# Sums of squares of each attention head's output: a row of ones as weights, or the squares as weights

## The chip, the core and the metric

One program on one NeuronCore of a Trainium2 chip; the other cores are idle. The metric is the device time of the whole program in microseconds, a median over several executions. The engines are PE (matrix multiply, with its weight loads shown apart as PEld), DVE (vector), ACT (scalar activation), POOL (GpSimd) and SP (which issues DMAs); each works through its own queue in order, and semaphores tie them together.

## The reference

One encoder layer on 1024 tokens of width 1024: RMSNorm, a combined projection into a pooling branch and eight heads of differential attention, gates, an output projection, and an MLP with squared ReLU. What matters here is the end of attention:

```python
o = lax.map(block, (q_blocks, q_pos))             # softmax0 @ v - lam * softmax1 @ v
o = o.transpose(1, 0, 2, 3, 4).reshape(B, S, N_HEADS, V_HEAD_DIM)
o = head_rmsnorm(o, g_sub) * (1.0 - lambda_init)
```

For each token and head, `head_rmsnorm` needs the mean of the squares of the head's 128 output channels. The rest of the layer is as usual:

```python
merged = (gates[..., :D_MODEL] * (y_pool @ w_branch_pool[l])
          + gates[..., D_MODEL:] * (y_attn @ w_branch_attn[l]))
x = x + merged @ w_out[l]
x = x + jnp.square(jax.nn.relu(h2 @ w_up[l])) @ w_down[l]
```

## The kernel before

All products keep fp32 accuracy by splitting each operand into a high part, rounded to the fp32r type, and a low part, the remainder (`split`, L118: a cast on ACT, a subtraction on DVE or POOL); `mm3` (L123) adds three fp32r matmuls for each product. Transposes go through PE as well, with the identity matrix `identf`.

The first 700 us are the attention stage. For each head h (8) and each tile t of 128 tokens (8), a chain of small generators runs: A makes q, k, v (`z`, 24 matmuls of 384 columns), B normalizes them, C transposes q and k, D makes the scores and the softmax, E transposes the attention weights, and for each pair p of tiles F multiplies them with v and H sums the squares. The table `ORDER` (L50, L51) interleaves the stages of neighbouring tiles in the order in which they are written; after that, the framework's scheduler lays every engine's queue out anew from its priorities and its own model of time. Matmuls of the gates and of the pooling branch (`g`, `u`) have lower priority and fill the gaps between.

`stage_pv` (L539) leaves a head's output, transposed, for 256 tokens in the PSUM bank `po`: partitions are the head's 128 channels, columns 0 to 255 one partial sum and 256 to 511 the other. There is one such bank. ACT copies the second half to `oS` (L558), DVE adds the first (L559), ACT squares it into `oq` (L560), and `oS` is stored to DRAM (L561). `split` then makes two fp32r digits `oqs` of the squares (L563).

`stage_ssq` (L567) sums over the channels, which lie on partitions, by a matmul: the weights are the 128x128 tile `ones`, the digits are streamed (L570, L571, 256 columns each), so that every partition of the second half of `po` holds the same row of 256 sums. To get them as columns, with tokens on partitions, DVE multiplies each 128x128 block with the identity and adds up along the row (L573, twice, each followed by a read of its accumulator) into the table `SS[h]`. When a head is done, `stage_norm` (L580) makes the factors from `SS[h]` and transposes and stores them; the factors are used only after the attention stage. For the last tile of the last head, H and R get a later priority (L642, L643).

From 700 us on follow the branch projections, the gates, the output projection and the MLP, the two larger ones by a Strassen-like scheme of seven products; the change doesn't touch them.

Of the kernel before, what the change touches and what calls it, by code (L numbers as in the profile page):

```python
# [9 lines left out]
F32R = mybir.dt.float32r  # L10
I32 = mybir.dt.int32
AF = mybir.ActivationFunctionType
ALU = mybir.AluOpType
# [4 lines left out]
P = 128  # L18
# [40 lines left out]
def encoder_kernel(  # L59
# [21 lines left out]
    nc = tc.nc  # L81
    x, out = x[0], out[0]
# [32 lines left out]
    def f(ap):  # L115
        return ap.bitcast(F32)

    def split(hi, lo, src, lo_eng=None):  # L118

        nc.scalar.copy(hi, src)  # L120
        return (lo_eng or nc.vector).tensor_tensor(lo, src, f(hi), op=ALU.subtract)  # L121
# [91 lines left out]
    identf = units.tile([P, P], F32, name="identf")  # L213
# [3 lines left out]
    ones = units.tile([P, P], F32R, name="ones")  # L217
# [57 lines left out]
    with ExitStack() as ph:  # L275
# [6 lines left out]
        def s1(shape, dt, name, tag, bufs=1):  # L282
            return sq_pool.tile(shape, dt, tag=tag, name=name, bufs=bufs)
# [107 lines left out]
        st = {}  # L391
        ATs = {}
        Zs = {}
        SS = {}
# [144 lines left out]
        def stage_pv(h, p):  # L539
            V, rooms = KV[h][1], ATs.pop((h, p))  # L540
            po = ps_o.tile([P, 512], F32, tag="o", name=f"po{h}_{p}")
            both = po.rearrange("p (d c) -> p d c", d=2)
            nkt = 2 * p + 2
            order = [*range(nkt - 2), nkt - 1, nkt - 2] if p else [0, 1]
            for i, kt in enumerate(order):
                v_hi, v_lo = (V[kt // 4][:, kt % 4, d, :] for d in range(2))
                a = rooms[kt // 2][:, :, kt % 2, :]
                if kt < nkt - 1:
                    nc.tensor.matmul(both, v_hi, a, start=i == 0, stop=False)
                    nc.tensor.matmul(po[:, 0:256], v_lo, a[:, 0, :], start=False, stop=i == nkt - 1)  # L550
                else:
                    for v in (v_hi, v_lo):
                        nc.tensor.matmul(both[:, :, P:256], v, a[:, :, P:256], start=False, stop=i == nkt - 1 and v is v_lo)
                if i % 2 and i < nkt - 1:
                    yield
            oS = s1([P, 256], F32, f"oS{h}_{p}", "oS", 2)
            oq = s1([P, 256], F32, f"oq{h}_{p}", "oq")
            nc.scalar.copy(oS, po[:, 256:512])  # L558
            nc.vector.tensor_tensor(oS, po[:, 0:256], oS, op=ALU.add)  # L559
            nc.scalar.activation(oq, oS, AF.Square)  # L560
            nc.scalar.dma_start(y_dram[h * P : (h + 1) * P, p * 256 : (p + 1) * 256], oS)  # L561
            oqs = s1([P, 2, 256], F32R, f"oqs{h}_{p}", "oqs")
            split(oqs[:, 0, :], oqs[:, 1, :], oq)  # L563
            st[h, p, "o"] = (po, oq, oqs)
            yield

        def stage_ssq(h, p):  # L567

            po, oq, oqs = st.pop((h, p, "o"))
            nc.tensor.matmul(po[:, 256:512], ones, oqs[:, 0, :], start=True, stop=False)  # L570
            nc.tensor.matmul(po[:, 256:512], ones, oqs[:, 1, :], start=False, stop=True)  # L571
            for i in range(2):
                nc.vector.tensor_tensor_reduce(  # L573
                    out=oq[:, i * P : (i + 1) * P], in0=po[:, 256 + i * P : 256 + (i + 1) * P], in1=identf,
                    scale=1.0, scalar=0.0, op0=ALU.mult, op1=ALU.add,
                    accum_out=SS[h][:, 2 * p + i : 2 * p + i + 1],
                )
            yield

        def stage_norm(h):  # L580
# [19 lines left out]
        def stage(w, g):  # L600
            h, t = divmod(g, NT)
            if w == "A":
                if t == 0:
                    head_start(h)
                yield from stage_qkv(h, t)
            elif w == "B":
                yield from stage_prep(h, t)
            elif w == "C":
                yield from stage_qkT(h, t)
            elif w == "D":  # L610
                yield from stage_scores(h, t)
            elif w == "E":
                yield from stage_aT(h, t)
            elif w == "F" and t % 2:
                yield from stage_pv(h, t // 2)
            elif w == "H" and t % 2:
                yield from stage_ssq(h, t // 2)
            elif w == "R" and t == NT - 1:
                yield from stage_norm(h)
            elif w == "W" and t == 0 and h:  # L620
                for kp in range(NK // 2):
                    load_w(h, kp)
                    split_w(h, kp, nc.gpsimd)

        for g in range(-2, N + 8):
# [11 lines left out]
            for tok in ORDER:  # L637
                if tok not in gens:
                    i = g - tok[1]
# [897 lines left out]
```

## Time and profile before

| | us |
|---|---|
| median of 3 executions (1526.28 to 1529.02) | 1528.49 |
| the profiled execution's own time | 1528.55 |
| its span in the trace | 1526.7 |
| PE busy | 1510.5 |
| PE weight loads (PEld) busy | 1301.4 |
| DVE busy | 1051.1 |
| ACT busy | 803.5 |
| POOL busy | 321.3 |
| first and last of the sums' matmuls (L570, L571) start at | 77.5 and 689.4 |

A row of the timeline gives the start, the time taken, the engine, the line in the program, the operation, what it writes and reads by the names of the program's tiles, and the shapes. "x4" is four in close order, whose time runs from the start of the first to the end of the last. A matmul's time includes its way through the array, which overlaps with the next one, so how far an instruction moves the next one is read from the difference of start times. A weight load (PEld) stands ahead of each matmul and can run beside the matmul before it. In the list of waits, "PE sc L484 <- DVE nm L487: 0.5, 1, 0.5" says that PE sat idle before L484 for 0.5 us in all, once, 0.5 at most, and that DVE's L487 ended it. In the view of one tile, three numbers after the count are the shortest, the median and the longest duration in ns.

### The profile page before, as it was taken

What the parts mean: (1) busy time and instruction counts of PE and PEld (TensorE: products, weight loads), DVE (VectorE), ACT (ScalarE), POOL (GpSimd) and SP (SyncE); (2) the same over time, 40 slices, a digit from 0 to 9 for tenths busy, and PEclk for the clock granted to TensorE, in tenths of its full rate; (3) what the DMA queues carried; (4) which work ended last, traced back from release to release, by engine and by line L of the source; (5) the groups of instructions that cost most, each with busy time, mean ns of one, the idle gap of its engine ahead of it and who ended that gap; (6) DMA issues with size and microseconds to landing.
All of it is one profiled execution on the core that took longest, in us unless ns stands there. A gap on an engine that the chain in (4) does not pass through costs nothing.

```text
span 1526.7 us, 21670 instructions
## 1 busy us (share of the span) xinstructions
PE 1510.5 (99%) x7441; PEld 1301.4 (85%) x7441; DVE 1051.1 (69%) x2262; ACT 803.5 (53%) x1693; POOL 321.3 (21%) x412
## 2 busy tenths in 40 slices
PE   7999999999999999999999999999999999999998
PEld 6999998999898989888888887888888888888887
DVE  7776768877777777746578569766665668556572
ACT  6665556656566565454464466555555633333331
POOL 6687333325234242312100011000000000000000
PEclk9999999999999999999999999999999999999999
DMA  8353211112112121626365734554433799537650
GB/s 247 103 161 121 72 34 57 52 42 68 43 44 84 49 98 37 226 86 242 135 207 188 253 111 140 173 178 152 151 125 111 278 363 366 166 125 262 226 193 28
DMA packets 171608, 221.07 MB, mean 145 GB/s; under 512 B 10902, under 2 KB 104811, under 8 KB 171499
## 3 DMA queue, kind: packets, MB, share of 16 engines
q1 hardware_dynamic: 154090, 192.39, 38.1%
q10 hardware_dynamic: 17408, 27.30, 4.7%
q8 instruction: 59, 0.97, 0.3%
q14 instruction: 51, 0.41, 0.1%
HBM read 157.76 MB, written 61.90 MB: 144 GB/s over the span
## 4 chain that ended last, share of the span: by engine, by line
PE 92%; DVE 4%; DMA 1%; ACT 1%; SPq 1%; issue 1%; DVEq 0%; ACTq 0%
PE z L126 6%; PE z L128 6%; PE z L127 5%; PE Da L126 4%; PE Da L128 4%; PE Da L127 4%; PE g L126 4%; PE g L127 4%; PE g L128 4%; PE Db L128 3%; PE Db L126 3%; PE Db L127 3%; PE X L128 2%; PE X L126 2%; PE X L127 2%; PE sc L484 2%
## 5 line engine op out<-in xcount | busy, mean ns | idle before, releaser
L126 PE MATMUL z<-wqkv,hT 128*128 128x384 f32 x512 | 174.7, 342 | 0.7 <-DVE qn L428 0.4
L128 PE MATMUL z<-wqkv,hT 128*128 128x384 f32 x512 | 173.7, 340 | 0.0
L127 PE MATMUL z<-wqkv,hT 128*128 128x384 f32 x512 | 173.6, 339 | 0.0
L495 ACT ACTIVATE s<-s,nm 128x256 f32<-128x256 f32 (+7 forms) x128 | 99.5, 778 | 45.9 <-DVE nm L487 45.1
L126 PE MATMUL g<-hT,fwgate 128*128 128x512 f32 x256 | 101.1, 395 | 0.1
L127 PE MATMUL g<-hT,fwgate 128*128 128x512 f32 x256 | 100.8, 394 | 0.0
L128 PE MATMUL g<-hT,fwgate 128*128 128x512 f32 x256 | 100.5, 393 | 0.0
L126 PEld LDWEIGHTS z<-wqkv,hT 128*128 128x128 f32 x512 | 96.8, 189 | 3.9 <-DVE qn L428 1.1
L127 PEld LDWEIGHTS z<-wqkv,hT 128*128 128x128 f32 x512 | 96.8, 189 | 3.0
L128 PEld LDWEIGHTS z<-wqkv,hT 128*128 128x128 f32 x512 | 96.7, 189 | 2.6 <-DVE hT L121 0.5
L235 POOL TENSOR_TENSOR ms<-ms,mhalf 128x4 f32<-128x4 f32 x64 | 65.7, 1027 | 156.6 <-DVE ms L234 133.6
L121 DVE TENSOR_TENSOR AT<-ta,AT 128x256 fp32r<-128x256 f32 (+1 forms) x160 | 62.2, 392 | 31.6 <-ACT AT L120 30.6
L487 DVE CUSTOM_DVE_ANT_0 s<-sc,dist 128x512 f32<-128x512 f32 (+3 forms) x128 | 74.0, 584 | 13.7 <-PE sc L485 12.5
L120 ACT CAST AT<-ta 128x256 fp32r<-128x256 f32 (+1 forms) x160 | 54.6, 348 | 38.4 <-PE ta L527 21.6
L484 PE MATMUL sc<-K,Q 128*128 128x512 f32 (+2 forms) x192 | 69.8, 366 | 0.6 <-DVE nm L487 0.5
L121 DVE TENSOR_TENSOR AS<-s,AS 128x512 fp32r<-128x512 f32 x64 | 45.1, 706 | 35.8 <-ACT AS L120 35.6
L485 PE MATMUL sc<-K,Q 128*128 128x512 f32 (+2 forms) x192 | 66.4, 350 | 0.0
L121 POOL TENSOR_TENSOR wqkv<-rqkv,wqkv 128x384 fp32r<-128x384 f32 x60 | 61.8, 1046 | 18.9 <-ACT wqkv L120 15.4
L121 POOL TENSOR_TENSOR fwgate<-frgate,fwgate 128x512 fp32r<-128x512 f32 x32 | 43.0, 1345 | 66.7 <-ACT fwgate L120 60.6
L126 PEld LDWEIGHTS g<-hT,fwgate 128*128 128x128 f32 x256 | 48.1, 188 | 9.4 <-ACT go L730 0.5
L128 PEld LDWEIGHTS g<-hT,fwgate 128*128 128x128 f32 x256 | 48.1, 188 | 8.9
L127 PEld LDWEIGHTS g<-hT,fwgate 128*128 128x128 f32 x256 | 48.1, 188 | 8.4
(455 smaller groups left out, 4489.7 us busy)
## 6 DMA issues: line engine op xcount, KB each, us to landing
wd<-in_w_down_dram SPq DMA_DIRECT2D x56, 512.0 KB, 5.6
wu<-in_w_up_dram SPq DMA_DIRECT2D x32, 512.0 KB, 4.7
udS<-us SPq DMA_DIRECT2D x64, 256.0 KB, 2.4
ur<-udS SPq DMA_DIRECT2D x32, 512.0 KB, 3.3
rqkv<-in_w_in_dram SPq DMA_DIRECT2D x64, 192.0 KB, 2.7
ud<-u ACTq DMA_DIRECT2D x48, 256.0 KB, 4.6
ur<-ud SPq DMA_DIRECT2D x24, 512.0 KB, 4.6
frgate<-in_w_gate_dram SPq DMA_DIRECT2D x32, 256.0 KB, 2.7
```

Source lines behind the costliest of these rows:

```text
L120: nc.scalar.copy(hi, src)
L121: return (lo_eng or nc.vector).tensor_tensor(lo, src, f(hi), op=ALU.subtract)
L126: nc.tensor.matmul(ps, lhs_hi, rhs_hi, start=first, stop=False, **kw)
L127: nc.tensor.matmul(ps, lhs_hi, rhs_lo, start=False, stop=False, **kw)
L128: nc.tensor.matmul(ps, lhs_lo, rhs_hi, start=False, stop=last, **kw)
L235: nc.gpsimd.tensor_tensor(dst, dst, mhalf[:, :n], op=ALU.pow)
L484: nc.tensor.matmul(dst, Q[:, i, 0, :], rhs, start=True, stop=False)
L485: nc.tensor.matmul(dst, Q[:, i, 1, :], rhs, start=False, stop=True)
L487: nc.vector.tensor_tensor_reduce(out=s[i][:, c : c + w], in0=sc[:, 0:w], in1=dist[:, o0 + c : o0 + c + w], scale=2.0 ** -(h + 1), scalar=B ...
L495: nc.scalar.activation(s[i][:, 0:n], s[i][:, 0:n], AF.Exp, bias=last, scale=-1.0, accum_out=Z[:, i, t : t + 1])
```

## The change

The squares `oq` are no longer split: they are used as they are, in fp32, and as the stationary operand. For each of the two tiles of a pair, one matmul has a 128x128 block of the squares as its weights and one column of `ones` (as fp32) as its moving operand. Channels are summed and tokens come out on partitions, one column for each tile, in columns 256 and 257 of `po`. One DVE copy of 128x2 moves them into `SS[h]`. The tile `oqs`, the two digits, the masked reductions and their accumulator reads are gone.

```diff
             nc.scalar.dma_start(y_dram[h * P : (h + 1) * P, p * 256 : (p + 1) * 256], oS)
-            oqs = s1([P, 2, 256], F32R, f"oqs{h}_{p}", "oqs")
-            split(oqs[:, 0, :], oqs[:, 1, :], oq)
-            st[h, p, "o"] = (po, oq, oqs)
+            st[h, p, "o"] = (po, oq)
             yield
 
         def stage_ssq(h, p):
 
-            po, oq, oqs = st.pop((h, p, "o"))
-            nc.tensor.matmul(po[:, 256:512], ones, oqs[:, 0, :], start=True, stop=False)
-            nc.tensor.matmul(po[:, 256:512], ones, oqs[:, 1, :], start=False, stop=True)
+            po, oq = st.pop((h, p, "o"))
             for i in range(2):
-                nc.vector.tensor_tensor_reduce(
-                    out=oq[:, i * P : (i + 1) * P], in0=po[:, 256 + i * P : 256 + (i + 1) * P], in1=identf,
-                    scale=1.0, scalar=0.0, op0=ALU.mult, op1=ALU.add,
-                    accum_out=SS[h][:, 2 * p + i : 2 * p + i + 1],
+                nc.tensor.matmul(
+                    po[:, 256 + i : 257 + i], oq[:, i * P : (i + 1) * P], f(ones)[:, 0:1], start=True, stop=True
                 )
+            nc.vector.tensor_copy(SS[h][:, 2 * p : 2 * p + 2], po[:, 256:258])
             yield
```

Because the scheduler sees other instructions, it lays the queues of the whole attention stage out differently. Two places show it. The first is PE at the first sum, head 0 and tiles 0 and 1 (`po_0` is the bank of that pair, `sc` a score bank, `ta` the transposed attention weights, `g` a gate, `z` a projection). Before:

```order
L128 MATMUL g_0_6794<-hT_0_0_156,fwgate_1_6791 128x512
L484 MATMUL sc_4_1_0_937<-K_0_366,Q_4_779 128x512
L485 MATMUL sc_4_1_0_937<-K_0_366,Q_4_779 128x512
L570 MATMUL po_0_803<-oqs_0_814,ones 128x256
L527 MATMUL ta_3_0_919<-identf,s_3_786 128x128 x4
L484 MATMUL sc_4_1_512_941<-K_1_367,Q_4_779 128x256
L571 MATMUL po_0_803<-oqs_0_814,ones 128x256
L485 MATMUL sc_4_1_512_941<-K_1_367,Q_4_779 128x256
L126 MATMUL z_0_1024<-wqkv_0_820,hT_0_0_150 128x384
```

And now, with L569 the new matmul:

```order
L128 MATMUL g_0_6666<-hT_0_0_156,fwgate_1_6663 128x512
L569 MATMUL po_0_803<-ones,oq_0_809 128x1 x2
L484 MATMUL sc_4_1_0_933<-K_0_366,Q_4_779 128x512
L527 MATMUL ta_3_0_915<-identf,s_3_786 128x128 x4
L485 MATMUL sc_4_1_0_933<-K_0_366,Q_4_779 128x512
L484 MATMUL sc_4_1_512_937<-K_1_367,Q_4_779 128x256
L485 MATMUL sc_4_1_512_937<-K_1_367,Q_4_779 128x256
L126 MATMUL z_0_1020<-wqkv_0_817,hT_0_0_150 128x384
```

The two sums stood apart, each with 256-wide or wider neighbours; now they stand together, ahead of the scores instead of behind them. The second place is DVE at the same sum, where the result is read (`SS` is the table of sums, `nm` and `s` belong to the scores). Before:

```order
L487 ISA s_4_1_913,nm_4_914<-sc_4_1_0_937,dist 128x512
L487 ISA nm_4_914 128x1
L573 ISA oq_0_809,SS_371<-po_0_803,identf 128x128
L573 ISA SS_371 128x1
L487 ISA s_4_1_913,nm_4_914<-sc_4_1_512_941,dist,nm_4_914 128x128
L487 ISA nm_4_914 128x1
L121 TENSOR_TENSOR AT_1_0_793<-ta_3_0_919,AT_1_0_793 128x2x128
```

The two rows of L573 stand there twice, once for each tile. Now, with L572 the new copy:

```order
L572 COPY SS_371<-po_0_803 128x2
L487 ISA s_4_1_909,nm_4_910<-sc_4_1_0_933,dist 128x512
L487 ISA nm_4_910 128x1
L121 TENSOR_TENSOR AT_1_0_793<-ta_3_0_915,AT_1_0_793 128x2x128
L487 ISA s_4_1_909,nm_4_910<-sc_4_1_512_937,dist,nm_4_910 128x128
L487 ISA nm_4_910 128x1
```

Four instructions have become one, and the reading of the sums now stands ahead of the first score reduction (L487, 512 columns) instead of between the two.

## The prediction

> **What bounds the kernel now.** I read the page first: the busy shares, the 40 slices and the chain that ended last.
>
> ```profile
> span 1526.7 us, 21670 instructions
> ...
> PE 1510.5 (99%) x7441; PEld 1301.4 (85%) x7441; DVE 1051.1 (69%) x2262; ACT 803.5 (53%) x1693; POOL 321.3 (21%) x412
> ...
> PE   7999999999999999999999999999999999999998
> ...
> PE 92%; DVE 4%; DMA 1%; ACT 1%; SPq 1%; issue 1%; DVEq 0%; ACTq 0%
> ```
>
> TensorE (PE) is busy in every slice after the first, and 92% of the chain is PE. A busy PE need not be a full PE, because matmuls overlap in this view. So I read next the sums by stretch for the attention stage, where all edited lines run, and the list of what PE itself waited for.
>
> ```profile
> core 0: us, PE busy (x) PEld busy (x) DVE busy (x) ACT busy (x) POOL busy (x), PEclk, DMA share, GB/s
> ...
> 100.00:200.00 100.00, 99.85 (x565) 91.91 (x564) 71.53 (x225) 55.50 (x151) 55.17 (x75) 1.00 0.30 96
> ...
> 500.00:600.00 100.00, 99.46 (x561) 90.49 (x560) 77.31 (x237) 57.29 (x157) 32.70 (x39) 1.00 0.18 62
> ```
>
> ```profile
> PE hps L261 <- DVE hn L256: 9.0, 1, 9.0
> ...
> PE sc L484 <- DVE nm L487: 0.5, 1, 0.5
> PE z L126 <- DVE qn L428: 0.4, 1, 0.4
> ```
>
> The clock is 1.00 throughout. PE's one long wait (9.0 us) is at the very start, before the edited lines run; in the attention stage the list has only 0.5 and 0.4 us. DVE is busy 72 to 77% of a stretch and ACT 55 to 57%. So here PE's instruction stream sets the time: what matters is how far each instruction pushes the next one back, not how long one lasts. That is read from start times, at the first place where the sums run (PE alone):
>
> ```profile
> 77.09 0.39 PE L484 MATMUL sc<-K,Q 128*128 128x512 f32 x1
> 77.32 0.39 PE L485 MATMUL sc<-K,Q 128*128 128x512 f32 x1
> 77.55 0.28 PE L570 MATMUL po<-oqs,ones 128*128 128x256 f32 x1
> 77.67 0.60 PE L527 MATMUL ta<-identf,s 128*128 128x128 f32 x4
> 78.02 0.36 PE L484 MATMUL sc<-K,Q 128*128 128x256 f32 x1
> 78.22 0.28 PE L571 MATMUL po<-oqs,ones 128*128 128x256 f32 x1
> 78.34 0.28 PE L485 MATMUL sc<-K,Q 128*128 128x256 f32 x1
> 78.46 0.34 PE L126 MATMUL z<-wqkv,hT 128*128 128x384 f32 x1
> ```
>
> A 512-wide matmul holds the stream for 0.23 us (77.32 to 77.55), a 256-wide one for 0.12 (78.22 to 78.34, and 78.34 to 78.46). The weight loads of the same place stand beside them:
>
> ```profile
> 77.55 0.48 PEld L527 LDWEIGHTS ta<-identf,s 128*128 128x128 f32 x4
> 78.00 0.19 PEld L484 LDWEIGHTS sc<-K,Q 128*128 128x128 f32 x1
> 78.11 0.19 PEld L571 LDWEIGHTS po<-oqs,ones 128*128 128x128 f32 x1
> ```
>
> **What a weight load costs.** This is the number on which the change turns. Under a 512-wide matmul a load is hidden. The four transposes of L527 and the 256-wide L484 behind them run from 77.67 to 78.22, 0.55 us; less 0.12 for L484 that is 0.43, or 0.11 for each transpose. Their matmul part is shorter than that: L484 is stamped 0.02 us after its own load began (78.00), yet the next matmul starts 0.20 after it and not 0.12, so L484 had to wait for its weights, and the loads follow each other at 0.11 (78.00 to 78.11). I read 0.11 us as the pace of a 128x128 weight load that has no long matmul to hide under.
>
> **PE: what goes.** L570 and L571 run 32 times each (8 heads, 4 pairs of tiles): 64 matmuls of 256 columns at 0.12 us = 7.7 us, all on PE's stream and so on the path. Each had one load, hidden by its own 256 columns or a neighbour's.
>
> **PE: what comes.** Now the squares are the weights and one column of ones is streamed. The order of PE's queue shows 64 matmuls of shape 128x1, two for each pair of tiles, side by side. These are true fp32, where the removed ones were fp32r. The built program of the changed kernel holds 7505 matmuls and as many weight loads, against 7441 of each on the page: 64 more, with 64 removed and 64 written, so each of the written ones is built as two loads with a matmul each. That makes 128 loads in groups of four. The trace of before has no fp32 matmul that isn't a transpose. The nearest row is the group of four transposes above: fp32 weights of 128x128 behind each other, with little to stream. One column can't hide a load, so 4 x 0.11 = 0.44 us for each pair of tiles where 2 x 0.12 = 0.24 stood: 128 x 0.11 = 14.1 us in, 7.7 out, **+6.4 us**. The load in front of the group hides under the matmul before it, but the load of the matmul behind it doesn't, so four are paid.
>
> From below: if each written matmul cost one load, 64 x 0.11 = 7.0, net -0.7. From above there is the one small matmul of the trace, the 32-column transpose of L371:
>
> ```profile
> 41.67 0.40 PE L128 MATMUL g<-hT,fwgate 128*128 128x512 f32 x1
> 42.00 0.24 PE L371 MATMUL cols_ps<-identf,rows 32*128 32x32 f32 x1
> 42.17 0.65 PE L261 MATMUL hps<-identf,hn 128*128 128x128 f32 x4
> ```
>
> It holds the stream 0.17 us (42.00 to 42.17). At that price 128 x 0.17 = 21.8, net +14.1. I take 0.11: 128 columns of fp32 weights in close order are what the change makes, L371 loads 32 rows and comes alone behind a wait.
>
> The Trainium skill ("FP8 and Floating Point Precision", TensorE Precision Notes) says that true fp32 takes four passes through the array, high and low halves crossed. If every pass reloaded the weights, four loads would stand for each written matmul where the sum counts two, and this is a rival below. No run here shows it yet.
>
> **DVE and ACT.** Gone, with the conversion of the squares into two digits and the masked reduction:
>
> ```profile
> L120 ACT CAST oqs<-oq x32: 387/406/462, 73.2 to 684.0; 128x256 fp32r<-128x256 f32 x32
> L121 DVE TENSOR_TENSOR oqs<-oq,oqs x32: 406/425/1320, 74.3 to 684.8; 128x256 fp32r<-128x256 f32 x32
> ...
> L573 DVE CUSTOM_DVE_ANT_0 oq<-po,identf x64: 272/285/292, 78.5 to 691.8; 128x128 f32<-128x128 f32 x64
> ```
>
> ACT loses 32 x 0.41 = 13 us; DVE loses 32 x 0.43 + 64 x 0.29 = 32 us. What comes is 32 copies of 128x2 out of PSUM. The nearest row is the 128x24 copy:
>
> ```profile
> L372 DVE COPY cols<-cols_ps x1: 183/183/183, 42.3 to 42.3; 128x24 f32<-128x24 f32 x1
> ```
>
> 32 x 0.18 = 6 us. All of it lies beside PE's stream, which neither engine holds up by more than the 0.5 and 0.4 us above: I count it at nothing. The weight-load list has a little more of such waits:
>
> ```profile
> PEld sc L484 <- DVE nm L487: 1.6, 4, 0.7
> ...
> PEld z L126 <- DVE qn L428: 1.1, 3, 0.4
> ```
>
> Were all of it cured, 1.6 + 1.1 = 2.7 us is the most that relief can bring; the same waits can as well grow, since the scheduler has laid out the whole stage anew. Between -2.7 and +2.7 I take 0.
>
> **The waits that are added or shortened.** On PE the sum now waits for ACT's square instead of DVE's low digit; PE takes its instructions in order, so a late square would stop all behind it. The scheduler has used the shorter chain to place the sums earlier: between the last product into a po bank and the sum on it stand 21 to 37 matmuls in the changed order (14 to 45 before). At a mean of about 0.18 us (100 us over 565 in the stretch above) 21 are some 3.8 us. How late the square can be shows at the worst place of the trace:
>
> ```profile
> 634.03 0.28 PE L550 MATMUL po<-AT,V 128*128 128x256 f32 x1
> ...
> 639.76 0.40 ACT L560 ACTIVATE oq<-oS 128x256 f32<-128x256 f32 x1
> ```
>
> There it ends 5.85 us after the product (640.16 less 634.31); one with 21 matmuls ahead would cost PE 2 us there, but the usual one comes much earlier:
>
> ```profile
> 209.24 0.28 PE L550 MATMUL po<-AT,V 128*128 128x256 f32 x1
> ...
> 211.12 0.42 ACT L560 ACTIVATE oq<-oS 128x256 f32<-128x256 f32 x1
> ```
>
> 2.0 us. I count 0, with one or two such stops (2 to 4 us) inside the range. On DVE the 128x2 copy waits for PE where the reduction did; the score reductions (L487) are queued behind it, and PE's next scores wait for those; where the reduction stood behind the first of them, the copy now stands ahead, so a late sum would hold up both. But the sum itself comes earlier, and the copy is shorter (6 us in all against 64 x 0.29 = 19), so I count 0. The single po bank comes free earlier, and the order already has other work ahead of the next product.
>
> **Sum.** The profiled execution took 1528.55 us (span 1526.7, the rest around it), 0.06 from the median of 1528.49. 1528.55 - 7.7 + 14.1 = **1535.0 us**. I take 0.2% (3 us) as what a measurement can tell from no change: 1525.4 to 1531.5.
>
> **Rivals.**
> - *One load's worth each* (ends not slower): the two loads of one written matmul overlap, so that a pair of tiles pays two and not four. 1528.55 - 0.7 = 1527.9. It decides at 0.06 us a load (7.7 / 128): below that the change costs nothing. For it: none of the loads of before is true fp32. Against: the transposes' loads do not overlap (0.11 apart).
> - *That, and PE's small waits vanish*: 1527.9 - 2.7 = 1525.2, just faster. For it: DVE loses 26 us net and the sums' chain two steps. Against: 0.9 us is all that PE's own list has in this stage.
> - *Loads that don't run in close order*: 0.17 each as at L371, 1528.55 + 14.1 = 1542.7. For it: a column so short leaves load and matmul nothing to overlap, and true fp32 stands amid fp32r. Against: L371 had a wait in front of it.
> - *Four loads for each written matmul*: 256 x 0.11 = 28.2, less 7.7, +20.5: 1549.1. Against: the built program has two.
>
> **Chances and range.** Forecast 0.58 (1532 to 1539 with the stops and the relief), one load's worth 0.15, that with cured waits 0.06, loads not in close order 0.13, four loads 0.08. The range takes in the forecast, most of the first rival and the third: 1527.8 to 1543.5. Faster by over 0.2%: 0.06. Within 0.2%: the first rival, and 0.03 of the forecast for loads a little cheaper together with full relief, 0.18. Slower: 0.76.
>
> **What would show it.** Right: four loads 0.11 apart at each sum, PE's next matmul some 0.45 us behind the first of them, PE's waits in the attention stage still about 1 us, and the end of the last sum some 6 us later while the stages behind it keep their lengths. DVE's busy time falls by about 26 us and that buys nothing. Wrong: loads at 0.06 or less; a sum that pushes the next matmul back by 0.7 us or more; waits of PE on the squares (L560) or of the scores on DVE that sum to several us; or a later stage that changes its length.

## The result, and the profile after

The changed kernel takes 1537.93 us (median of 6, 1536.96 to 1543.04) where the kernel before took 1528.76 on the same occasions (6 runs, 1526.28 to 1529.68): a ratio of 1.007, interval 1.0058 to 1.0081, or 9.2 us more. The profiled execution took 1536.96 us, 8.4 above the profiled one of before. The page of the changed kernel, the lines that answer to those of before:

```profile
span 1535.1 us, 21661 instructions
...
PE 1515.2 (99%) x7505; PEld 1306.6 (85%) x7505; DVE 1018.9 (66%) x2134; ACT 795.9 (52%) x1661; POOL 317.2 (21%) x412
...
PE 93%; DVE 3%; ACT 1%; DMA 1%; issue 1%; SPq 1%; POOL 0%; ACTq 0%; DVEq 0%
```

PE carries the chain as before. DVE has lost 32.2 us of busy time and ACT 7.6, and the span has grown by 8.4. The view of the tile `po` shows the new sums:

```profile
L569 PEld LDWEIGHTS po<-ones,oq x128: 186/191/192, 76.1 to 659.1; 128*128 128x128 f32 x128
L569 PE MATMUL po<-ones,oq x128: 164/250/250, 76.4 to 659.1; 128*128 128x1 f32 x128
...
L572 DVE COPY SS<-po x32: 140/152/160, 76.9 to 659.4; 128x2 f32<-128x2 f32 x32
```

128 loads for the 64 matmuls written, so two each. How they hold PE's stream shows in the timeline at the first sum, PE and then its loads:

```profile
76.14 0.40 PE L128 MATMUL g<-hT,fwgate 128*128 128x512 f32 x1
76.38 0.50 PE L569 MATMUL po<-ones,oq 128*128 128x1 f32 x4
76.74 0.48 PE L484 MATMUL sc<-K,Q 128*128 128x512 f32 x1
77.06 0.60 PE L527 MATMUL ta<-identf,s 128*128 128x128 f32 x4
```

```profile
76.15 0.64 PEld L569 LDWEIGHTS po<-ones,oq 128*128 128x128 f32 x4
76.71 0.19 PEld L484 LDWEIGHTS sc<-K,Q 128*128 128x128 f32 x1
```

From 76.38 to 77.06 are 0.68 us. They hold the four small matmuls and one of 512 columns, which alone takes 0.23: 0.45 is left for the four. L484 starts 0.03 us after its own load has begun and then lasts 0.32 instead of 0.23, as it did behind the four transposes of before: the fourth load is paid there. The same reading at each of the 30 places where the four stand together gives a median of 0.45 us too. 32 x 0.45 = 14.4 us come, 7.7 go: 6.7 us.

The other 1.7 us of the span's 8.4 aren't in the attention stage. The first and last starts of three groups mark the ends of the stages; kernel before, then changed (`bp` is the first projection behind attention, `X` the first product of the MLP's up-projection, `Da` the first of its down-projection):

```profile
L126 PE MATMUL bp<-ypT,wbp x64: 387/389/390, 696.8 to 739.8; 128*128 128x512 f32 x64
L126 PE MATMUL X<-B11h,A x64: 389/389/476, 910.0 to 1186.5; 128*128 128x512 f32 x64
L126 PE MATMUL Da<-w_0h,u_0h x32: 389/389/499, 1217.1 to 1483.8; 128*128 128x512 f32 x32
```

```profile
L126 PE MATMUL bp<-ypT,wbp x64: 389/389/389, 702.8 to 745.7; 128*128 128x512 f32 x64
L126 PE MATMUL X<-B11h,A x64: 388/389/476, 915.8 to 1194.9; 128*128 128x512 f32 x64
L126 PE MATMUL Da<-w_0h,u_0h x32: 389/389/499, 1225.5 to 1492.1; 128*128 128x512 f32 x32
```

| stretch | before | changed | difference |
|---|---|---|---|
| start to `bp` (attention) | 696.8 | 702.8 | +6.0 |
| `bp` to `X` | 213.2 | 213.0 | -0.2 |
| `X` to `Da` (up-projection) | 307.1 | 309.7 | +2.6 |
| `Da` to the end | 309.6 | 309.6 | 0 |

So the attention stage grew by the loads less 0.7, and a stage that the change doesn't touch grew by 2.6 us. PE's list of waits in the changed kernel says where:

```profile
PE hps L261 <- DVE hn L256: 10.3, 2, 9.0
PE hb L1106 <- POOL y L1103: 1.7, 2, 1.0
PE X L126 <- ACT U L1269: 1.5, 1, 1.5
PE sc L484 <- DVE nm L487: 1.3, 2, 1.0
...
PE z L126 <- DVE qn L428: 0.2, 1, 0.2
```

The wait of `X` for ACT is new, and that of `hb` for POOL has grown; in the list of before it is

```profile
PE hb L1111 <- POOL y L1108: 0.5, 1, 0.5
```

Together the two grew by 2.7 us, against 2.6 for the stage, and they stand where the up-projection begins. One reading was at hand: the scheduler had ordered the start of the MLP differently. The experiments test it.

Some kernels below have two groups of executions 5 us apart (of the six of the changed kernel, two lie at 1542 to 1543); what sets them apart is told in the last section.

### The profile page after: what moved, and what is told of

It reads as the page before. It is cut to its first block, busy times and chain, and to the rows that moved or that the text cites. A ratio compares the mean times of both kernels' runs of the same rounds, so it can differ in the third digit from the quotient of the medians.

```text
span 1535.1 us, 21661 instructions
## 1 busy us (share of the span) xinstructions
PE 1515.2 (99%) x7505; PEld 1306.6 (85%) x7505; DVE 1018.9 (66%) x2134; ACT 795.9 (52%) x1661; POOL 317.2 (21%) x412
## 4 chain that ended last, share of the span: by engine, by line
PE 93%; DVE 3%; ACT 1%; DMA 1%; issue 1%; SPq 1%; POOL 0%; ACTq 0%; DVEq 0%
PE z L126 6%; PE z L128 6%; PE z L127 6%; PE Da L126 4%; PE Da L127 4%; PE Da L128 4%; PE g L126 4%; PE g L127 4%; PE g L128 4%; PE Db L127 3%; PE Db L128 3%; PE Db L126 3%; PE X L126 2%; PE X L127 2%; PE X L128 2%; PE sc L484 2%
## 5 line engine op out<-in xcount | busy, mean ns | idle before, releaser
L487 DVE CUSTOM_DVE_ANT_0 s<-sc,dist 128x512 f32<-128x512 f32 (+3 forms) x128 | 74.3, 584 | 12.0 <-PE sc L485 11.3
L484 PE MATMUL sc<-K,Q 128*128 128x512 f32 (+2 forms) x192 | 70.9, 371 | 1.3 <-DVE nm L487 1.3
```

Source lines behind the costliest of these rows:

```text
L484: nc.tensor.matmul(dst, Q[:, i, 0, :], rhs, start=True, stop=False)
L487: nc.vector.tensor_tensor_reduce(out=s[i][:, c : c + w], in0=sc[:, 0:w], in1=dist[:, o0 + c : o0 + c + w], scale=2.0 ** -(h + 1), scalar=B ...
```

## The experiments

Two theories were to be told apart, with a third kept in sight. **Loads**: every weight load that stands behind another holds the stream 0.11 us, whatever its type, and the attention stage grows by their number. **True fp32**: it is the type, not the count. **New order**: the scheduler lays all queues out anew, and that alone is worth some us.

**One load for each matmul.** The squares are rounded to one fp32r digit and used as weights (two columns of ones are streamed):

```diff
-            oq = s1([P, 256], F32, f"oq{h}_{p}", "oq")
+            oq = s1([P, 256], F32R, f"oq{h}_{p}", "oq")
...
-                    po[:, 256 + i : 257 + i], oq[:, i * P : (i + 1) * P], f(ones)[:, 0:1], start=True, stop=True
+                    po[:, 256 + 2 * i : 258 + 2 * i], oq[:, i * P : (i + 1) * P], ones[:, 0:2], start=True, stop=True
```

> The changed kernel with the squares rounded to one fp32r digit (the low digit is left out of the sums), so that each of the 64 matmuls should need one weight load and not two; two columns of ones are streamed instead of one. Theory of the loads: 64 x 0.11 = 7.0 us come and 7.7 go, the attention stage ends within 1 us of the kernel before, and the time is 1528 to 1530 us. Rival, the newly laid out order and its stops: the order is as new as in the changed kernel, so about 1535 to 1538. Rival, relief of DVE and ACT counts for something: 1525 to 1526.

Measured: 1527.91 us (seven of twelve executions at 1527.0 to 1528.0, five at 1532.3 to 1533.2), ratio 1.0008, interval 0.9998 to 1.0019. PE at the first sum:

```profile
75.41 0.28 PE L569 MATMUL po<-ones,oq 128*128 128x2 f32 x2
75.55 0.48 PE L126 MATMUL g<-hT,fwgate 128*128 128x512 f32 x1
75.87 0.39 PE L127 MATMUL g<-hT,fwgate 128*128 128x512 f32 x1
```

75.41 to 75.87, less 0.23, leaves 0.23 us for two loads, against 0.24 for the two wide matmuls of before. Half the loads, and the rise is gone. The attention stage ended at 692.7, 4.1 us earlier than before, where 1 us at most was expected: PE starts 0.4 earlier, and behind the first 45 us its stops of over 0.15 us come to 0.5 us where they came to 2.5; the rest is spread over small differences and wasn't traced further. `X` to `Da` took 309.6, as in the changed kernel and 2.5 more than before. That the time came out so near the forecast is in part luck: the stops that went and the order of the MLP nearly cancel.

**Four loads without true fp32.** The two fp32r digits of before, used as weights:

```diff
-            nc.tensor.matmul(po[:, 256:512], ones, oqs[:, 0, :], start=True, stop=False)
-            nc.tensor.matmul(po[:, 256:512], ones, oqs[:, 1, :], start=False, stop=True)
+            for i in range(2):
+                for d in range(2):
+                    nc.tensor.matmul(
+                        po[:, 256 + 2 * i : 258 + 2 * i], oqs[:, d, i * P : (i + 1) * P], ones[:, 0:2],
+                        start=d == 0, stop=d == 1,
+                    )
...
+            nc.vector.tensor_copy(SS[h][:, 2 * p : 2 * p + 2], po[:, 256:260:2])
```

The masked reductions of DVE give way to the one copy, as in the changed kernel.

> Squares as weights, but as the two fp32r digits of the kernel before (cast and subtraction are kept), so that four loads stand at each sum as in the changed kernel, none of true fp32. Theory of the loads: the stream is held 0.45 us at each sum, the attention stage ends 6 us later than in the kernel before, 1534.5 to 1538 us. Rival, that true fp32 itself is dear: no rise, 1527 to 1530.

Measured: 1535.36 us (five executions, 1533.77 to 1535.53), ratio 1.0041, interval 1.0029 to 1.0053. True fp32 is not needed for the rise: fp32r loads in fours cost it too. Here the scheduler put another group into the four, which shows what one of them is worth:

```profile
78.86 0.39 PE L572 MATMUL po<-ones,oqs 128*128 128x2 f32 x3
79.11 0.37 PE L485 MATMUL sc<-K,Q 128*128 128x256 f32 x1
79.31 0.34 PE L126 MATMUL z<-wqkv,hT 128*128 128x384 f32 x1
```

78.86 to 79.31 is 0.45 us for three of them and a 256-wide matmul of 0.12: 0.33, or 0.11 each. Attention ended at 701.5, 4.7 us later than before, where the loads make 6.7, and 8.8 later than with one digit, where 64 more loads make 7.0: the stops differ by some 2 us each time. The two kernels with one and two digits have the same order from the start of the MLP on, and both took 309.5 to 309.6 us from `X` to `Da`.

**Twice the loads.** Each of the changed kernel's matmuls done twice, adding into the same column:

```diff
-                nc.tensor.matmul(
-                    po[:, 256 + i : 257 + i], oq[:, i * P : (i + 1) * P], f(ones)[:, 0:1], start=True, stop=True
-                )
+                for d in range(2):
+                    nc.tensor.matmul(
+                        po[:, 256 + i : 257 + i], oq[:, i * P : (i + 1) * P], f(ones)[:, 0:1],
+                        start=d == 0, stop=d == 1,
+                    )
```

> The changed kernel with each of its 64 matmuls done twice (the sums come out doubled, nothing else is left out), so that eight loads stand at each sum. The order of the MLP's start is nearly that of the kernel before here, so only the loads should count. Theory of the loads: 256 x 0.11 = 28.2 us come and 7.7 go, the attention stage ends 20 us later than before, about 1549 us. Rival, a cost for each sum and not for each load (a wait, a change between fp32r and fp32): as the changed kernel or little above, 1535 to 1540.

Measured: 1555.25 us (four executions, 1552.45 to 1555.73), ratio 1.0169, interval 1.0155 to 1.0183. The rise goes with the number of loads, not of sums. PE at the first sum:

```profile
76.97 0.95 PE L570 MATMUL po<-ones,oq 128*128 128x1 f32 x8
77.78 0.63 PE L527 MATMUL ta<-identf,s 128*128 128x128 f32 x4
78.17 0.48 PE L484 MATMUL sc<-K,Q 128*128 128x512 f32 x1
78.48 0.39 PE L485 MATMUL sc<-K,Q 128*128 128x512 f32 x1
```

76.97 to 78.48 are 1.51 us; less 0.23 for the 512 columns, 1.28 are left for eight small matmuls and four transposes, 0.11 each. Attention ended at 721.4, 24.6 us later than before, and `X` to `Da` took 307.1, as before. The rise is 4 to 6 us more than the 20.5 that the loads explain, and PE's waits name much of it:

```profile
PE ta L527 <- DVE s L504: 2.1, 1, 2.1
PE po L570 <- ACT oq L560: 0.9, 1, 0.9
PE g L126 <- ACT yps L719: 0.8, 1, 0.8
PE trr L588 <- POOL r L586: 0.6, 1, 0.6
```

The 2.1 us before L527 come from the slow DVE instruction of the last section (L503 took 5.88 us here). Without the four stops, 4.4 us, 1548 would be left of the profiled execution's 1552.45, beside the 1549 that were expected.

**Relief alone.** PE as before, DVE and ACT as changed (the high digit is streamed twice, and two columns of the rows are copied):

```diff
-            for i in range(2):
-                nc.tensor.matmul(
-                    po[:, 256 + i : 257 + i], oq[:, i * P : (i + 1) * P], f(ones)[:, 0:1], start=True, stop=True
-                )
+            nc.tensor.matmul(po[:, 256:512], ones, oq, start=True, stop=False)
+            nc.tensor.matmul(po[:, 256:512], ones, oq, start=False, stop=True)
```

> PE's stream as in the kernel before (two matmuls of 256 columns with ones as weights at each sum, the high digit streamed twice), but DVE and ACT as in the changed kernel: no digits, no masked reductions, one copy of 128x2, so that what lands in the table of sums is not the sums of the tokens. Theory of the loads: DVE loses some 26 us of busy time and the time stays, 1527.5 to 1530 us. Rival, relief counts: 1525 to 1526. Rival, the newly laid out order costs 2 us or more by itself: 1530 to 1533.

Measured: 1531.59 us (five of twelve executions at 1526.0 to 1527.8, seven at 1531.4 to 1533.2), ratio 1.001, interval 0.9998 to 1.0021. The page of this kernel beside the marks of its stages:

```profile
PE 1509.9 (99%) x7441; PEld 1302.1 (85%) x7441; DVE 1021.5 (67%) x2134; ACT 794.5 (52%) x1661; POOL 315.6 (21%) x412
```

```profile
L126 PE MATMUL bp<-ypT,wbp x64: 388/389/390, 696.1 to 739.0; 128*128 128x512 f32 x64
```

DVE is 29.6 us less busy, and in this execution (1527.84 us) the attention stage ends 0.7 us earlier. The lower five have a median of 1527.0, 1.6 us below the kernel before, so that is the most that relief can have bought; over all twelve it bought nothing. The median lies in the range of the second rival, a dearer order, but the upper seven lie 3.5 us and more above the lower five, like the upper groups of other kernels, and none of them was profiled: what lifts them stays open.

**Another order of the MLP, sums as before.** One number of the order table (the norm of a head one place later) makes the scheduler order PE's matmuls from `bp` on exactly as in the changed kernel, while the sums stay:

```diff
-O = "B1 C2 H6 D3 R7 E4 F5 W-2 A0"
+O = "B1 C2 H6 D3 R8 E4 F5 W-2 A0"
```

> The kernel before with the same number altered by one (R8 for R7); by this the scheduler orders the start of the MLP as it does in the changed kernel, while the sums stay as they were. Theory of two parts: the stretch from the first up-projection to the first down-projection rises from 307.1 to about 309.6 us, and the time is 1530.5 to 1532 us. Rival, the order of the MLP is worth nothing: 1528 to 1529.

Measured: 1531.85 us (11 executions, 1530.4 to 1533.69), ratio 1.0022, interval 1.0013 to 1.003.

```profile
PE X L126 <- ACT U L1274: 1.8, 1, 1.8
PE hb L1111 <- POOL y L1108: 1.7, 2, 1.0
```

```profile
L126 PE MATMUL X<-B11h,A x64: 388/389/476, 909.1 to 1188.5; 128*128 128x512 f32 x64
L126 PE MATMUL Da<-w_0h,u_0h x32: 389/389/500, 1219.1 to 1485.8; 128*128 128x512 f32 x32
```

The same two waits appear, and `X` to `Da` grows to 310.0 us with no change to the sums at all. The 2.6 us belong to the order.

**The changed kernel with the other MLP order.** With R9 for R7 the changed kernel gave no result. With the edit of the experiment before this one, R8 for R7, its MLP has nearly the order of the kernel before:

> The changed kernel with R8 for R7 in the order table; by this the scheduler orders the start of the MLP nearly as in the kernel before, and the sums and their loads stay as changed. Theory of two parts (6.4 us of loads in the attention stage, 2.5 us from another order at the start of the MLP): the stretch from the first up-projection to the first down-projection falls from 309.7 to about 307.2 us, and executions without the long DVE instruction take 1534 to 1536 us. Rival, all 9 us come from the edit itself: 1537 to 1538.

Measured: 1540.52 us (two of six executions at 1536.2 and 1536.4, four at 1540 to 1542.7), ratio 1.0075, interval 1.0062 to 1.0087. `X` to `Da` (922.7 to 1229.8) took 307.1: that part came out as expected. The time did not: the median lies above both ranges, and the two lower executions 0.2 and 0.4 us above the range of the first theory. The profiled one, at 1541.07, is of the upper ones (L503 took 6.77 us) and shows what the attention stage, laid out anew once more, has in stops of its own:

```profile
PE ta L527 <- DVE s L504: 3.0, 1, 3.0
PE sc L484 <- DVE nm L487: 1.5, 3, 0.5
PE yp L126 <- ACT go L725: 1.1, 1, 1.1
```

The 3.0 us are the slow instruction's, and 3.4 us at half clock behind them cost 1.7 more. Without both, 1536.4 us are left, as the lower two executions have.

**Less work on PE.** One fp32r digit, streamed against the ones as in the kernel before, one matmul for each sum instead of two. With one digit the split goes too, so ACT loses its cast and DVE its subtraction:

```diff
-            nc.tensor.matmul(po[:, 256:512], ones, oqs[:, 0, :], start=True, stop=False)
-            nc.tensor.matmul(po[:, 256:512], ones, oqs[:, 1, :], start=False, stop=True)
+            nc.tensor.matmul(po[:, 256:512], ones, oq, start=True, stop=True)
```

> The kernel before with the squares rounded to one fp32r digit (the low digit is left out): one matmul of 256 columns at each sum instead of two, ones as weights, DVE's masked reductions kept. Theory of the loads (what counts is how long PE's stream is held): 32 x 0.12 = 3.8 us go, about 1524.7 us, the attention stage ends 3.8 us earlier. Rival, stops of the new order: anywhere between 1524 and 1530, with stops seen in PE's list of waits.

Measured: 1523.71 us (seven of twelve executions at 1521.9 to 1524.0, five at 1526.6 to 1528.6), ratio 0.9975, interval 0.9965 to 0.9985: 0.25% faster than the kernel before; only this edit and its variant below are. It leaves the low digit out of the sums. The lower seven lie 0.7 to 2.8 us below the 1524.7 that were expected. The profiled execution is of the upper five; its attention stage ended at 696.0 with the stop and the half clock of the last section in it, so the 3.8 us can't be read there.

**The same with R8**, to regain what the MLP's order costs:

> One fp32r digit streamed against the ones, as in the third experiment (the low digit is left out), with R8 for R7, by which the start of the MLP is ordered nearly as in the kernel before. Theory: 3.8 us less in the attention stage, up to 1 us less in the MLP than the third experiment, 1522 to 1525 us in executions without the long DVE instruction. Rival, the attention stage is laid out anew again and its stops take back a part: 1525 to 1528.

Measured: 1524.27 us (seven executions, 1521.92 to 1530.1), ratio 0.997, interval 0.9959 to 0.9981. No different from the one before it: the 0.3 us that `X` to `Da` gained (307.6 against 307.9) don't show. (The profiled execution is the slowest of the seven; L503 took 6.24 us in it.)

**One digit as weights with H7 for H6**, again for the MLP's order:

> One fp32r digit of the squares as weights, as in the first experiment (the low digit is left out), with H7 for H6, by which the start of the MLP is ordered almost as in the kernel before. Theory of two parts: the first experiment loses its 2.5 us in the MLP, 1524.5 to 1526.5 us in executions without the long DVE instruction. Rival, the attention stage that is laid out anew takes them back: 1527 to 1529.

Measured: 1528.28 us (11 executions, 1524.63 to 1532.23), ratio 0.9999, interval 0.999 to 1.0007. `X` to `Da` (909.6 to 1216.7) fell to 307.1 as expected, and two executions reached 1525; the profiled one, at 1528.11, has the long instruction of the last section (L503 took 6.75 us, `bp` at 696.6). It stops PE for 2.6 us and is followed by 3.4 us at half clock, 1.7 us more: without these 4.3 us, 1523.8 would be left.

**POOL's other work later.** This belongs to the two groups of executions: the branch weights are prepared later.

```diff
-PREP_AT = (2, 4, 6, 8)
+PREP_AT = (12, 14, 16, 18)
```

> The changed kernel with R8, and with POOL's preparation of the branch weights begun ten gate steps later, so that POOL is not busy without a gap around 82 us. Theory of the long DVE instruction (L503 waits some 6 us while POOL has one operation behind the other, PE stops and runs at half clock afterwards): no execution is 5 us above the others any more, all of them lie within 2 us of 1535. Rival, the 5 us come from something else: a third or more of the executions still lie at 1539 to 1541.

Measured: 1545.81 us (four executions, 1544.93 to 1548.16), ratio 1.012, interval 1.0105 to 1.0134. The executions now lie within 3.2 us of each other and L503 is nowhere long, but the level is 10 us above what was expected: with the order changed, PE ran out of work near the end of attention (a stop of 5.7 us at L527) and went on at half clock for 6.8 us. The experiment doesn't settle what makes the groups.

## Why the prediction was right, and where it was not

- **What bounds the stage**: right. PE's stream does; DVE lost 30 us in the relief kernel and the time stayed within 2 us. (The 72 to 77% given for DVE are those of the two stretches shown; from 100 to 700 us it is busy 59 to 78%.)
- **The price of a load**: right. 0.11 us was read from four transposes; the four fp32 loads hold the stream 0.45 us (0.44 forecast), three fp32r loads 0.33. In all these kernels a load comes with a small matmul of its own, so 0.11 us is the price of the two together; that it is the load is read from the wide matmul behind each group, which waits for its own load.
- **The number of loads**: right, two for each fp32 matmul (128 on PEld). One load each gave no rise; with twice the loads the attention stage ended 24.6 us later (20.5 by the sum, since the 7.7 us that go are the same, and 4.4 of stops that PE's list names). The four passes of true fp32 that the Trainium skill names ("FP8 and Floating Point Precision", TensorE Precision Notes) don't show as four loads.
- **The attention stage**: +6.0 us against +6.4, of which 6.7 are loads; the -0.7 that remains is put down to stops.
- **Relief and added waits at nothing**: right for relief, within the 1.6 us above. Of the waits, one stop of 1 us stands right behind a sum (L484 for DVE's L487), and others went; PE's list for the stage's matmuls is 1.3 and 0.2 us where 0.5 and 0.4 stood. DVE fell by 32.2 us and not 26, ACT by 7.6 and not 13: DVE's subtraction was costed at its median of 0.43 us, though some took up to 1.32; the copies took 0.15 each against 0.18, and the 64 accumulator reads (5.2 us), which the prediction doesn't count, ran beside other work. ACT's instructions, added up one by one, did fall by 12.8 us; its busy time fell by less because it counts a stretch in which two of them overlap only once.
- **"The stages behind it keep their lengths"**: this step failed. The up-projection grew by 2.6 us because the scheduler had ordered its start differently, and the kernel before does the same when it is given that order (+2.9 us). The edit in attention reaches the MLP through the scheduler alone. Just how the scheduler comes to it wasn't examined.

The sum was 6.4 us, and the profiled execution shows 8.4: 6.0 in attention, 2.6 in the up-projection, -0.2 between the two. That the time still fell between 1532 and 1539 is owed to the width that was left for stops, not to this part, which the sum put at nothing. The medians are 9.2 apart; without the two executions 5 us above the rest they are 8.7 apart, and that these two have the slow instruction of the last section is argued, since neither was profiled. None of the rivals came true; one load's worth each would have needed loads that cost 0.06 us or less, and here each holds the stream 0.11.

## What to carry to other kernels

In these runs a matmul cost PE's stream the longer of its columns and its weight load: 0.23 us for 512 columns of fp32r, 0.12 for 256, and 0.11 for 1 or 2 columns with a load of 128x128. So exchanging the operands to stream 1 column in place of 256 gains nothing, and weights in true fp32, which pay two loads, lose. When an engine is full, count what each instruction adds to its stream from start times, and let relief of the other engines count for nothing until a wait names them. Where a scheduler orders the whole program, compare the lengths of the stages that an edit doesn't touch, and price the order by giving it to the kernel without the edit.

## What the runs showed of the hardware that was not expected

Five of the twelve profiles have one slow DVE instruction in common; four of the five are of executions 3.5 to 8 us above the lowest of their kernel, and the fifth is the one with twice the loads. In the profile of the kernel with one digit streamed, taken at 1527.95 us, DVE and POOL at 81 us:

```profile
80.94 0.17 DVE L502 RECIPROCAL cf<-Z 128x1 f32<-128x1 f32 x1
81.14 6.34 DVE L503 SCALAR_TENSOR_TENSOR cf<-cf,Z,nlam 128x1 f32<-128x1 f32 x1
87.51 0.94 DVE L504 SCALAR_TENSOR_TENSOR s<-s,cf,s 128x640 f32<-128x640 f32 x1
```

```profile
80.64 0.74 POOL L760 TENSOR_TENSOR wd<-wq,wd 128x256 fp32r<-128x256 f32 x1
81.35 1.01 POOL L121 TENSOR_TENSOR wqkv<-rqkv,wqkv 128x384 fp32r<-128x384 f32 x1
...
86.74 0.71 POOL L760 TENSOR_TENSOR wd<-wq,wd 128x256 fp32r<-128x256 f32 x1
87.54 0.38 POOL L400 TENSOR_SCALAR ggh<-gg 128x64 f32<-128x64 f32 x1
```

L503 works on 128x1 and takes 0.69 us at the same place of the changed kernel's profile. Here it took 6.34: POOL had ten operations one behind the other, the last ended at 87.45, and L503 ended at 87.48. The Trainium skill ("SBUF — State Buffer", section "SBUF: two separate sides") says that, when a DVE operation reads two inputs from SBUF and a GpSimd operation reads SBUF too, the pair of ports that both share is locked for a whole instruction by whichever comes first, and that the other is blocked meanwhile. The trace agrees (L503 reads `cf` and `Z`), and suggests that a row of POOL operations can keep DVE out for several of them. The other profiles fit: of the 768 executions of L503 in the twelve, 144 took over 0.35 us, and every one of these ended within 0.03 us behind the end of a POOL operation. The rest took about 0.22 us, 223 of them with a POOL operation running when they began, so not every one holds it up. That POOL is the cause was not shown by taking its work away. PE then pays twice:

```profile
88.51 1.11 PE L527 MATMUL ta<-identf,s 128*128 128x128 f32 x4 [2.91 <-DVE s L504]
...
90.06 0.52 PE L128 MATMUL z<-wqkv,hT 128*128 128x384 f32 x1
90.38 0.52 PE L126 MATMUL z<-wqkv,hT 128*128 128x384 f32 x1
```

```profile
86.00:88.00 2.00, 0.00 (x0) 0.00 (x0) 1.96 (x2) 0.00 (x0) 1.84 (x5) 0.90 0.54 161
88.00:94.40 6.40, 5.89 (x19) 5.70 (x20) 4.58 (x13) 2.96 (x8) 2.56 (x4) 0.50 0.45 155
94.40:100.00 5.60, 5.60 (x34) 5.35 (x34) 4.03 (x17) 2.75 (x8) 0.83 (x1) 1.00 0.01 3
```

It waits 2.9 us, and then runs at a granted clock of 0.50 until 94.4 us: 384-wide matmuls are 0.32 us apart instead of 0.17. 2.9 us of waiting and some 3 of half speed are the 5 to 6 us. The half clock lasted as long, 6.8 us, with R8; it lasted 3.4 us behind the stops of 3.0 and 2.6 us in the changed kernel with R8 and in the kernel with one digit as weights and H7, and did not come behind the stop of 2.1 us with twice the loads. Of the executions that weren't profiled only the mean clock is known: with one digit as weights it is 0.998 in all five of the upper group, and 0.999 or 1.000 in the seven lower ones. The kernel before has the instruction too (0.55 us in its profile), and only one of its 29 executions beside the first experiments lay 3 us high.
